# A hybrid decoder layer on one core: 24 transpositions of the identity ahead of the first rows

## The chip, the core and the metric

The kernel runs on one core of one Trainium2 chip. A core has five engines that run side by side, each through its own list of instructions, and wait for one another by semaphores: TensorE (PE) for matrix products and transpositions, its weight loads shown as PEld; VectorE (DVE) and ScalarE (ACT) for work on rows; GpSimd (POOL); and SyncE (SP), which here issues the transfers between DRAM and the on-chip memory SBUF. PE writes into PSUM, which has eight banks of 128 x 512 float32. The metric is the time of one execution on the device in microseconds (us).

## The reference

One decoder layer over 1024 positions of 1024 channels, with 16 learned "meta" rows put in front, all in float32:

```python
h = concat([meta, x])
hn = rms_norm(h, norm1_gain)
q, k, v, u = split(hn @ w_in)            # 512, 512, 512, 1024 columns
attn = diff_attention(q, k, v, ...)      # 4 heads, causal: softmax_1 - lam * softmax_2
conv = conformer_conv(u, ...)            # GLU, causal depthwise conv of 31 taps, LayerNorm, swish
h = h + concat([attn, conv]) @ w_out
a = relu(rms_norm(h, norm2_gain) @ w_up)
h = h + (a * a) @ w_down
return h[16:]
```

## The kernel before

Every matrix product is done on pairs: a float32 operand is split into a high part and a low part of the type that PE multiplies fast, and `three` (L317 to L321) issues high x high (L319), high x low (L320) and low x high (L321) into the same PSUM bank. The splitting takes ACT for the high part (L128 for activations, L138 for weights) and DVE for the low part (L129, L139).

At the start the rows come in as tiles: `mraw` with the 16 meta rows, and `xs` with eight tiles of 128 rows (L167, L215). `norm_tile` (L178) handles one: ACT squares the row and sums it (L182), POOL forms the reciprocal root (L124, L125), DVE scales the tile in place (L185), and PE transposes it in two halves of four 128 x 128 blocks each (L190, tile `xtr`, against the identity `ident`). Each half has a PSUM bank. The banks come from `trp`, a pool of two, but those of x tile 2 (`XPA`, L46) come from `pa`, the pool of six for products, tag `mm`. A bank is free again once ACT has copied its high part and DVE its low part (into `xm` for the meta rows, into `xT` for x). Meanwhile the weight rows `w_in` arrive in pieces `raw` of 128 x 512, with four buffers, and are split to `w`. The first products are `pu` (260 columns each: two x tiles and four meta columns), then `pq` for k, q and v, then the attention, the output projection and the feed-forward, whose second half (`py`, `px` with `pair`) fills the last third of the time.

`ident` is made by POOL at the very start (a memset and an affine_select in a helper, masks.py:197 and 199); all transpositions need it.

The order on each engine isn't that of the text. The kernel is recorded as it is written, and a scheduler then places the instructions on the engines by a model of their times (`schedule_with_timeline_sim=True`), within the limits that the pools' buffers and the data set. A new instruction can therefore move others, on any engine, anywhere behind it.

Of the kernel before, what the change touches and what calls it, by code (L numbers as in the profile page):

```python
# [9 lines left out]
F32 = mybir.dt.float32  # L10
# [6 lines left out]
P = 128  # L17
# [11 lines left out]
LATER = -200000  # L29
LOOK = 2  # L30
UQB = 2
FIN = 3
VPOS = (3,4)
APOSN = (3, 6)
# [25 lines left out]
def hybrid_layer_kernel(  # L60
# [18 lines left out]
    V, S, T, G = nc.vector, nc.scalar, nc.tensor, nc.gpsimd  # L79
# [9 lines left out]
    pa = ps_a.__enter__()  # L89
# [10 lines left out]
    def tr_bank(name):  # L100
# [7 lines left out]
    ident = cp.tile([P, P], F32, tag="ident", name="ident")  # L108
# [4 lines left out]
    G.memset(maskb, 0.0)  # L113
    G.affine_select(out=maskb, in_=maskb, compare_op=ALU.is_ge, fill=MASKED, base=0,
                    pattern=[[-1, P]], channel_multiplier=1)

    mhalf = cp.tile([P, 8], F32, tag="mhalf", name="mhalf")
    G.memset(mhalf, -0.5)
# [385 lines left out]
    def qstack(i, h, pool=None):  # L504
# [11 lines left out]
        for q in range(4):  # L516
            T.transpose(bank[:, q, :], qtf[:, q * P:(q + 1) * P], ident)
        uq = pool.tile([P, 4, P], F32R, tag=f"uq{h}", name=f"uq{h}") if pool else ap.tile([P, 4, P], F32R, tag="uq", name="uq", bufs=UQB)
        S.activation(uq, bank, AF.Copy)
# [231 lines left out]
    for n in range(-1, len(units) + BLAG):  # L751
# [20 lines left out]
        if n >= BLAG:  # L772
            i, h = units[n - BLAG]
            values(i, h, mixed.pop(0))
            if h == NH - 1:
                done.append((n + FIN, i, state["osb"], state["oss"]))
            if done and (n >= done[0][0] or n - BLAG == len(units) - 1):
# [457 lines left out]
```

## Time and profile before

| | us |
|---|---|
| three timed runs | 1132.49, 1133.85, 1135.59 |
| median | 1133.85 |
| the profiled execution | 1134.65 |
| its span, first to last instruction | 1132.5 |
| PE busy | 1098.7 (97%) |
| DVE busy | 814.8 (72%) |
| ACT busy | 618.5 (55%) |
| POOL busy | 142.3 (13%) |

All times below are counted from the first instruction of the profiled execution. PE's shares by stage tell where it waits; the waits themselves stand as "idle before, and what ended it" behind an instruction. An instruction's duration runs from its start to its end, and on PE, ACT and DVE the next one can start before that, so the distance of two starts is what a queue pays for one of them.

### The profile page before, as it was taken

Reading aid. Unit: us, or ns where it says so; the run is one execution under the profiler, and the core shown is the slowest. Engines: PE = TensorE matmul, PEld = TensorE weight load, DVE = VectorE, ACT = ScalarE, POOL = GpSimd, SP = SyncE. Lnnn points to the kernel's source line nnn. Section 1 sums busy time; section 2 is a strip of 40 time slices with the busy share of each in tenths; the row PEclk is TensorE's granted clock in tenths of the full one; section 3 lists DMA queues with packets and bytes.
Section 4 is the critical chain, followed back from the end, with each engine's and each line's share of the span. In section 5 each row is a group of like instructions: output and inputs, shape, how many; then the busy total and the mean of one; then the engine's idle time right before and its main releaser. Section 6 shows DMA issues by size and latency. Waiting matters only on the chain.

```text
span 1132.5 us, 15738 instructions
## 1 busy us (share of the span) xinstructions
PE 1098.7 (97%) x5696; PEld 925.3 (82%) x5696; DVE 814.8 (72%) x1354; ACT 618.5 (55%) x1379; POOL 142.3 (13%) x156
## 2 busy tenths in 40 slices
PE   6999999999999998997999999999999999999998
PEld 6999788877788877785888888878878888888887
DVE  7699899977888778689797878677657545356340
ACT  8521465447667676577767676676655333323320
POOL 3000564313001342250000000000000000000000
PEclk9999999999999999998999999999999999999999
DMA  7320011000222311384399996979399666465600
GB/s 269 118 76 1 1 38 38 29 10 19 75 71 97 131 66 57 110 271 140 130 330 322 311 339 238 331 252 328 148 340 384 245 256 219 190 229 201 220 38 37
DMA packets 87821, 189.92 MB, mean 168 GB/s; under 512 B 7472, under 2 KB 27184, under 8 KB 82112
## 3 DMA queue, kind: packets, MB, share of 16 engines
q1 hardware_dynamic: 87744, 188.92, 47.4%
q8 instruction: 44, 0.72, 0.3%
q14 instruction: 33, 0.27, 0.1%
HBM read 129.39 MB, written 59.51 MB: 167 GB/s over the span
## 4 chain that ended last, share of the span: by engine, by line
PE 81%; DVE 7%; DMA 5%; ACT 4%; issue 1%; POOL 1%; SPq 0%; POOLq 0%; DVEq 0%; ACTq 0%
PE px L321 7%; PE px L320 7%; PE px L319 7%; PE py L319 6%; PE py L320 6%; PE py L321 6%; PE pu L319 3%; PE pu L321 3%; PE pu L320 3%; PE pq L320 3%; PE pq L319 3%; PE pq L321 3%; PE ops L620 2%; PE pw L321 2%; PE pw L320 2%; PE pw L319 2%
## 5 line engine op out<-in xcount | busy, mean ns | idle before, releaser
L809 DVE TENSOR_TENSOR pair<-rv,pair 128x2048 fp32r<-128x2048 f32 x56 | 126.8, 2288 | 112.2 <-ACT pair L808 112.2
L808 ACT ACTIVATE pair<-rv 128x2048 fp32r<-128x2048 f32 x56 | 105.2, 1912 | 162.6 <-PE py L321 80.4
L319 PE MATMUL py<-pair 128*128 128x512 f32 x256 | 99.6, 389 | 0.0
L320 PE MATMUL py<-pair 128*128 128x512 f32 x256 | 99.6, 389 | 0.0
L321 PE MATMUL py<-pair 128*128 128x512 f32 x256 | 99.6, 389 | 0.0
L319 PE MATMUL px<-pair 128*128 128x512 f32 x192 | 74.8, 390 | 0.5 <-ACT pair L808 0.5
L320 PE MATMUL px<-pair 128*128 128x512 f32 x192 | 74.7, 389 | 0.0
L321 PE MATMUL px<-pair 128*128 128x512 f32 x192 | 73.8, 390 | 0.2 <-DVE pair L809 0.2
L320 PE MATMUL pu<-xT,w 128*128 128x260 f32 x256 | 72.1, 284 | 0.0
L319 PE MATMUL pu<-xT,w 128*128 128x260 f32 x256 | 71.4, 285 | 0.0
L321 PE MATMUL pu<-xT,w 128*128 128x260 f32 x256 | 71.4, 283 | 0.0
L894 ACT ACTIVATE wr<-wr,gains 128x256 f32<-128x256 f32 x128 | 54.8, 497 | 27.3 <-DMA wr<-in_w_up 26.7
L321 PEld LDWEIGHTS py<-pair 128*128 128x128 f32 x256 | 48.0, 188 | 10.1
L319 PEld LDWEIGHTS py<-pair 128*128 128x128 f32 x256 | 48.0, 188 | 10.0
L320 PEld LDWEIGHTS py<-pair 128*128 128x128 f32 x256 | 48.0, 188 | 9.9
L320 PE MATMUL px<-hnt,wp 128*128 128x512 f32 x128 | 51.1, 399 | 3.9 <-DVE hnt L809 3.9
L812 DVE TENSOR_TENSOR wdr<-wdr 128x1024 f32<-128x1024 f32 x32 | 39.1, 1221 | 20.4 <-DMA wdr<-in_w_down 20.2
L319 PE MATMUL px<-hnt,wp 128*128 128x512 f32 x128 | 50.7, 398 | 0.9 <-ACT sn L941 0.8
L321 PE MATMUL pq<-w,xT 128*128 128x512 f32 x128 | 50.9, 398 | 0.0
L319 PE MATMUL pq<-w,xT 128*128 128x512 f32 x128 | 50.9, 397 | 0.0
L320 PE MATMUL pq<-w,xT 128*128 128x512 f32 x128 | 50.8, 397 | 0.0
L321 PE MATMUL px<-hnt,wp 128*128 128x512 f32 x128 | 50.8, 397 | 0.0
(301 smaller groups left out, 3187.2 us busy)
## 6 DMA issues: line engine op xcount, KB each, us to landing
rv<-as SPq DMA_DIRECT2D x28, 1024.0 KB, 6.6
wr<-in_w_up SPq DMA_DIRECT2D x32, 512.0 KB, 5.0
as<-a SPq DMA_DIRECT2D x64, 256.0 KB, 4.9
wdr<-in_w_down SPq DMA_DIRECT2D x8, 2048.0 KB, 9.5
ws<-wdr SPq DMA_DIRECT2D x32, 512.0 KB, 4.4
rv<-ws SPq DMA_DIRECT2D x16, 1024.0 KB, 4.9
as<-as SPq DMA_DIRECT2D x48, 256.0 KB, 3.9
rv<-in_w_down SPq DMA_DIRECT2D x12, 1024.0 KB, 6.2
```

The source lines that it names most:

```text
L319: T.matmul(ps, st[0], mv[0], start=first, stop=False, skip_group_check=more)
L320: T.matmul(ps, st[0], mv[1], start=False, stop=False, skip_group_check=more)
L321: T.matmul(ps, st[1], mv[0], start=False, stop=last, skip_group_check=more)
L620: T.matmul(ops, u[:, 0, b, :], vb.rearrange("p a e -> p (a e)"), start=b == 0, stop=False)
L808: S.activation(hi, src, AF.Copy)
L809: (eng or V).tensor_tensor(out=lo, in0=src, in1=hi.bitcast(F32), op=ALU.subtract)
L812: eng.tensor_tensor(out=out, in0=a, in1=b, op=ALU.subtract)
L894: S.activation(r[:, k, :], r[:, k, :], AF.Copy, scale=gains[:, 1, 4 * j + k:4 * j + k + 1])
```

## The change

A constant `WAKE = 24` is added, and between the mask and `mhalf` in the setup a PSUM bank named `awake` is taken from `pa`, the pool of six. 24 transpositions of the identity by the identity, 128 x 128 in float32, are written into the four quarters of that bank in turn. Nothing reads it.

```diff
--- before.py
+++ after.py
@@ -29,6 +29,7 @@
 LATER = -200000
 LOOK = 2
 UQB = 2
+WAKE = 24
 FIN = 3
 VPOS = (3,4)
 APOSN = (3, 6)
@@ -113,6 +114,11 @@
     G.memset(maskb, 0.0)
     G.affine_select(out=maskb, in_=maskb, compare_op=ALU.is_ge, fill=MASKED, base=0,
                     pattern=[[-1, P]], channel_multiplier=1)
+
+
+    awake = pa.tile([P, 4, P], F32, tag="mm", name="awake")
+    for k in range(WAKE):
+        T.transpose(awake[:, k % 4, :], ident, ident)
 
     mhalf = cp.tile([P, 8], F32, tag="mhalf", name="mhalf")
     G.memset(mhalf, -0.5)
```

The changed file has these lines six further down (L190 of before is L196 of after). Names carry a buffer number that differs between the two builds; `xT_108` of before is `xT_133` of after, the pair of x tiles 0 and 1, and `w_186` is `w_211`, the first four weight pieces.

On PE the 24 stand at the head of the list, ahead of the meta rows' transpositions. The rows behind them are moved too. DVE before, from the scaling of x tile 0 to that of x tile 1 and three weight pieces:

```order
L185 TENSOR_SCALAR xs_102<-xs_102,rs 128x1024
L129 TENSOR_TENSOR xm<-xtr,xm 128x4x16 x2
L202 CAST xT_108<-xm 128x8x4
L202 CAST xT_109<-xm 128x8x4
L202 CAST xT_110<-xm 128x8x4
L202 CAST xT_111<-xm 128x8x4
L202 CAST xT_108<-xm 128x8x4
L202 CAST xT_109<-xm 128x8x4
L202 CAST xT_110<-xm 128x8x4
L202 CAST xT_111<-xm 128x8x4
L185 TENSOR_SCALAR xs_102<-xs_102,rs 128x1024
L139 SCALAR_TENSOR_TENSOR w_186<-raw,gains,w_186 128x512 x3
```

DVE after, the same part:

```order
L191 TENSOR_SCALAR xs_127<-xs_127,rs 128x1024
L145 SCALAR_TENSOR_TENSOR w_211<-raw,gains,w_211 128x512
L191 TENSOR_SCALAR xs_127<-xs_127,rs 128x1024
L145 SCALAR_TENSOR_TENSOR w_211<-raw,gains,w_211 128x512
L135 TENSOR_TENSOR xm<-xtr,xm 128x4x16
L145 SCALAR_TENSOR_TENSOR w_211<-raw,gains,w_211 128x512
L135 TENSOR_TENSOR xm<-xtr,xm 128x4x16
L208 CAST xT_133<-xm 128x8x4
L208 CAST xT_134<-xm 128x8x4
L208 CAST xT_135<-xm 128x8x4
L208 CAST xT_136<-xm 128x8x4
L145 SCALAR_TENSOR_TENSOR w_211<-raw,gains,w_211 128x512
```

The two copies of the meta rows' low parts (`xm`), which followed the scaling of x tile 0, now have one weight piece, x tile 1 and a second weight piece ahead of the first and a third piece ahead of the second; the eight casts come after, with the fourth piece among them. ACT is moved in the same way; before, from the Squares of the meta rows on:

```order
L182 ACTIVATE junk,ss<-mraw 16x1024
L182 ACTIVATE junk,ss<-xs_102 128x1024 x2
L128 ACTIVATE xm<-xtr 128x4x16 x2
L138 ACTIVATE w_186<-raw,gains 128x512 x3
L128 ACTIVATE xT_108<-xtr 128x4x128
L138 ACTIVATE w_186<-raw,gains 128x512
L128 ACTIVATE xT_108<-xtr 128x4x128
```

ACT after:

```order
L188 ACTIVATE junk,ss<-mraw 16x1024
L188 ACTIVATE junk,ss<-xs_127 128x1024 x2
L144 ACTIVATE w_211<-raw,gains 128x512 x2
L134 ACTIVATE xm<-xtr 128x4x16
L144 ACTIVATE w_211<-raw,gains 128x512
L134 ACTIVATE xm<-xtr 128x4x16
L144 ACTIVATE w_211<-raw,gains 128x512
L188 ACTIVATE junk,ss<-xs_127 128x1024
L134 ACTIVATE xT_133<-xtr 128x4x128 x2
```

The copies of `xm` stood behind the second x tile's Square; now two weight pieces stand ahead of the first and one between them, and the Square of x tile 2 is ahead of tile 0's copies. On SP the four pieces of the second half of these weights (L133), which followed all x tiles, now stand one by one between the x tiles 4 to 7.

Further on, up to the beginning of the feed-forward, rows are exchanged in many places on PE, DVE and ACT; in the last third the order is the same on all engines. One such place, in the attention, where the third block's result is transposed (`otr`, L640). PE before, with the last value products (`ops`) of a head ahead of it:

```order
L620 MATMUL ops<-vs_2913,u 128x256
L621 MATMUL ops<-vs_2913,u 128x128
L640 MATMUL otr<-ident,osb 128x128 x4
L517 MATMUL qtr<-ident,qt 128x128 x2
L607 MATMUL atr<-ident,pt 128x128
L517 MATMUL qtr<-ident,qt 128x128 x2
L620 MATMUL ops<-vm,u 128x256
L621 MATMUL ops<-vm,u 128x128
L620 MATMUL ops<-vs_2691,u 128x256
```

PE after, with the same `otr` in the eighth row:

```order
L523 MATMUL qtr<-ident,qt 128x128 x4
L544 MATMUL sps<-kst_1587,uq 128x264
L545 MATMUL sps<-kst_1587,uq 128x264
L544 MATMUL sps<-kst_1587,uq 128x264
L545 MATMUL sps<-kst_1587,uq 128x264
L547 LDWEIGHTS identb
L547 MATMUL sps<-maskb,identb 128x128
L646 MATMUL otr<-ident,osb 128x128 x4
L613 MATMUL atr<-ident,pt 128x128
L626 MATMUL ops<-vm,u 128x256
```

The output transposition now stands behind two groups of scores (`sps`); the query transpositions (`qtr`), which stood behind it on both sides of `atr`, have gone ahead.

## Rows read from the trace of the kernel before

**Rows 1.** The page: busy us, share of the span and instructions of each engine.

```profile
PE 1098.7 (97%) x5696; PEld 925.3 (82%) x5696; DVE 814.8 (72%) x1354; ACT 618.5 (55%) x1379; POOL 142.3 (13%) x156
```

**Rows 2.** Busy time by stage: stretch and length, engines, granted clock, DMA share, GB/s.

```profile
0.00:17.30 17.30, 8.06 (x38) 6.79 (x39) 11.35 (x33) 14.56 (x28) 7.72 (x23) 1.00 0.90 328
17.30:60.00 42.70, 42.70 (x361) 42.70 (x361) 32.35 (x71) 22.87 (x41) 2.92 (x6) 1.00 0.41 124
60.00:200.00 140.00, 140.00 (x851) 122.99 (x851) 132.46 (x238) 57.35 (x290) 49.41 (x28) 1.00 0.11 31
200.00:515.00 315.00, 301.51 (x1797) 253.41 (x1795) 252.44 (x568) 204.87 (x550) 82.27 (x99) 0.99 0.26 87
515.00:536.00 21.00, 15.26 (x54) 11.42 (x55) 19.92 (x28) 15.04 (x27) 0.00 (x0) 0.84 0.45 146
536.00:1132.50 596.50, 591.18 (x2603) 487.99 (x2602) 366.30 (x422) 303.84 (x446) 0.00 (x0) 1.00 0.67 242
```

**Rows 3.** Timeline of PE: start, length, line, tiles, count, idle before and releaser.

```profile
5.76 1.03 PE L190 MATMUL xtr<-ident,mraw 16*128 16x16 f32 x8 [5.76 <-DVE mraw L185]
8.01 1.97 PE L190 MATMUL xtr<-ident,xs 128*128 128x128 f32 x8 [1.22 <-DVE xm L129]
12.10 4.30 PE L190 MATMUL xtr<-ident,xs 128*128 128x128 f32 x16 [2.12 <-DVE xT L129]
16.05 1.22 PE L319 MATMUL pu<-xT,w 128*128 128x260 f32 x4
17.07 0.34 PE L320 MATMUL pu<-xT,w 128*128 128x260 f32 x1
```

**Rows 4.** Transpositions up to 20 us (min/median/max ns), and four later ones.

```profile
L190 PE MATMUL xtr<-ident,xs x32: 270/421/477, 8.0 to 19.9; 128*128 128x128 f32 x32
...
18.81 0.60 PE L190 MATMUL xtr<-ident,xs 128*128 128x128 f32 x4
```

**Rows 5.** Timeline of POOL, SP, ACT and DVE; the raw row is a DMA issue's landing.

```profile
1.17 0.29 POOL masks.py:199 TENSOR_SCALAR_AFFINE_SELECT ident<-ident 128x128 f32<-128x128 f32 x1
2.57 1.85 SPq L133 DMA_DIRECT2D raw<-in_w_in  x4
...
raw<-in_w_in SPq DMA_DIRECT2D x1, 256.0 KB, 5.0
...
7.36 0.32 ACT L128 ACTIVATE xm<-xtr 128x64 fp32r<-128x64 f32 x2
7.70 2.02 ACT L138 ACTIVATE w<-raw,gains 128x512 fp32r<-128x512 f32 x3
7.74 0.35 DVE L129 TENSOR_TENSOR xm<-xtr,xm 128x64 fp32r<-128x64 f32 x2
8.00 0.77 DVE L202 CAST xT<-xm 128x32 fp32r<-128x32 f32 x8
8.71 0.75 DVE L185 TENSOR_SCALAR xs<-xs,rs 128x1024 f32<-128x1024 f32 x1
9.38 2.07 DVE L139 SCALAR_TENSOR_TENSOR w<-raw,gains,w 128x512 fp32r<-128x512 f32 x3
11.36 0.68 DVE L129 TENSOR_TENSOR xT<-xtr,xT 128x512 fp32r<-128x512 f32 x1
14.29 0.22 DVE L269 TENSOR_TENSOR csum<-cw 128x60 f32<-128x60 f32 x1
```

**Rows 6.** Busy time in two pauses, columns as in rows 2.

```profile
399.00:403.00 4.00, 2.38 (x17) 1.76 (x17) 4.00 (x9) 2.65 (x6) 3.20 (x4) 0.99 0.24 90
403.00:406.40 3.40, 3.40 (x18) 3.29 (x18) 0.29 (x2) 3.15 (x12) 2.23 (x3) 0.52 0.00 0
526.80:530.80 4.00, 0.14 (x1) 0.00 (x0) 4.00 (x7) 1.93 (x4) 0.00 (x0) 0.80 0.72 232
530.80:536.00 5.20, 5.14 (x12) 4.12 (x13) 4.12 (x7) 2.34 (x6) 0.00 (x0) 0.50 0.49 159
```

**Rows 7.** PE's waits from 200 to 515, the longest single one: total, times, longest.

```profile
PE qtr L517 <- DVE msb L563: 1.7, 1, 1.7
```

## The prediction

> **What bounds the kernel now.** I read the page's busy shares first, then the busy time by stage, and then the first 20 us and two pauses instruction by instruction. TensorE (PE) is busy for 1098.7 of 1132.5 us [rows 1], so a change can give back at most the 33.8 us in which PE stands. The stages say where these lie: 17.30 - 8.06 = 9.24 us before 17.3 us, none from there to 200 us, 315.00 - 301.51 = 13.49 us in the attention (200 to 515), 21.00 - 15.26 = 5.74 us where the feed-forward begins (515 to 536), 596.50 - 591.18 = 5.32 us in all the rest [rows 2].
>
> The added work lies in the first of these stages, so what ends the waits there counts. PE waits for its first tile to be scaled until 5.76, for the first PSUM bank of the transpositions to be emptied by VectorE (DVE) until 8.01 and again until 12.10; its first product is issued at 16.05, and the first one that needs a low part (L320) at 17.07 [rows 3]. PE also runs at half pace there: eight transpositions take 1.97 us at 8.01, of which the last is 0.42 long, so (1.97 - 0.42) / 7, some 0.215 us apart; at 18.81 four take 0.60 us, so (0.60 - 0.27) / 3 = 0.11 us apart [rows 3, 4]. [...]
>
> **The change, part by part.** *The 24 transpositions.* They need the identity alone, which POOL has finished at 1.17 + 0.29 = 1.46 [rows 5]. At half pace they end at 1.5 + 24 x 0.215 = 6.7, at full pace at 1.5 + 24 x 0.11 = 4.1. The eight transpositions of the meta rows, which began at 5.76, so begin between 5.76 and 6.7, up to 0.9 us late. ScalarE (ACT) did not read them before the end of its second Square, near 7.4, and DVE not before 7.74 [rows 5], so by itself this costs nothing. The bank comes from the pool of six for products; its only writer is PE, which is long past it when the bank comes round: nothing, and at worst one wait for PE itself, which is in order anyway.
>
> *What they would give, if nothing else moved.* Between 12.10 and 17.2 PE ran 16 transpositions and 4 products at half pace, that is 16 x (0.215 - 0.11) = 1.65 us, and about half of the 1.02 us from 16.05 to 17.07, more than at full pace [rows 3, 4]. Together that is the end on the good side: -2.2 us.
>
> *The order.* The build's scheduler has placed everything anew, taking the meta rows to be late. On ACT two pieces of weights now go ahead of the first copy xm, and a third ahead of the second; on DVE likewise, with a scaling of xs in between. I walk this with the old durations. The first piece lands at 2.57 + 5.0 = 7.57 and ACT takes 2.02 / 3 = 0.67 us for each. DVE: weights 8.3 to 9.0, xs 9.0 to 9.7 (0.67 apart), weights 9.7 to 10.4, xm to 10.6 [rows 5]. Only then is the meta bank free, so x tile 0 is transposed from 10.6 (first half) and, one weight piece later, 11.4 (second half), where it was 8.01. Eight small casts (0.77) and the fourth piece (0.67) then hold DVE until 12.85, three tiny ones until about 13.1 (csum, one of that kind, takes 0.22 and they overlap), and the low part of tile 0's first half (0.68) ends at 13.75: tile 1 begins at 13.8, where it was 12.10. Then xs is scaled by 14.65, tile 2 is transposed from 14.7 (its bank is of the product pool), the second half of tile 0 is split until 15.3, and tile 1's second half follows tile 2. At full pace PE is through with these and with the four L319 at 16.5, at half pace at 18.2. The low part of tile 1's first half comes after csum, a weight piece and an xs (15.3 + 0.15 + 0.67 + 0.67, and 0.68 for itself) and ends at 17.45. So the first L320, which stood at 17.07 with the same work behind it, now stands at 17.5 with a full clock (+0.4) and at 18.2 with half a clock.
>
> *Which clock.* Between about 7.7 and 13.8 PE now has only eight transpositions, some 0.9 us of work. In the attention the clock fell while PE was busy for 2.38 of 4 us, and stood at 0.52 in the next 3.4 us; in the other pause it fell after PE had stood since 526.8, and read 0.50 from 530.8 to 536 [rows 6]. So whatever the 24 transpositions bring is probably given back before 13.8. Then PE works without a pause from 14.7. In the kernel before the pace doubled 17.2 - 16.05 = 1.15 us after the first product [rows 3]; at half pace the first product now stands at 17.2, so the same gives 18.4. That is half pace up to the first L320 at 18.2 and 0.2 us beyond, where before it was 0.1: 18.2 - 17.07 + (0.2 - 0.1) / 2, or +1.2 us.
>
> [...]
>
> For the start I take +0.8, between +0.4 and +1.2, with ends at -2.2 and, if the pace doubles some 1.5 us later still, +2.0. That no new wait follows rests on the cover after 17.3: PE was busy for all of 42.70 us, DVE for 32.35 and ACT for 22.87 [rows 2], so both have 10 us to spare. If a split of 0.68 us comes too late there, it costs that once or twice, at most 1.4 us.
>
> *SyncE's queue.* The second half's weight pieces now stand between the x tiles 4 to 7, one each, and each waits for its buffer, so a tile behind it is issued later. These tiles are used after 17.3, under the same cover: nothing, at most the 1.4 us already counted.
>
> *The attention and beyond.* There all queues have the same instructions in another order, transpositions and splits standing some rows earlier or later; from the feed-forward on the orders differ by single instructions, and the last third is the same. The 13.49 us of waits there are many short ones, the longest 1.7 us; the pause at 527, 4.00 - 0.14 us, lies behind it [rows 2, 6, 7]. I can derive no sign: 0, with one wait of 1.7 us either way as its usual size.
>
> The sum: the profiled execution took 1134.65 us, 2.15 more than its span, and lies 0.8 above the median of 1133.85. 1134.65 + 0.8 + 0 = 1135.45 on its scale, so 1133.85 + 0.8 = 1134.7 for the median. A difference of 0.3%, 3.4 us, is about what a measurement of this kernel can tell from none.
>
> **Rivals.** *The attention gets a pause more (slower).* The place is that of the kind at 399, where the output transpositions wait for DVE: 4.00 - 2.38 = 1.62 us standing and then 3.4 us at half clock, a loss of 1.7 [rows 6]. One more such place is +3.3, with the start's +0.8 and one wait of 1.7 it is 1133.85 + 5.8 = 1139.6; alone 1138.0. It decides once a wait is long or dense enough that the clock falls, since that doubles its price. For it: the new order puts these output transpositions right behind the scores, with no value products ahead of them. Against it: as many products are left to put elsewhere.
>
> *The attention loses that pause (faster).* In the same place the new order lets the value products of the earlier head go before. If the pause and the clock's fall go, and the longest wait of 1.7 too [rows 7]: 1133.85 + 0.8 - 3.3 - 1.7 = 1129.7. For it speaks only that the place is rearranged.
>
> *The clock rises early and stays (does what it says).* Then the start is worth between -2.2 and +0.4: 1131.7 to 1134.3, say 1133.0. Against it speak the six nearly idle microseconds.
>
> *The clock never notices the transpositions.* Then the first pieces run at half pace as walked above: 1133.85 + 1.2 = 1135.1. For it: PE was at half pace through all the transpositions from 5.76 on [rows 3]; against it: they had pauses of 1.22 and 2.12 us between them.
>
> **How the numbers follow.** The forecast, a start at +0.8 and an attention within 1.7 us, 0.45; clock early 0.08; clock unmoved 0.10; a pause more 0.22; a pause less 0.15. The first three lie within 0.3%, so 0.63 for no change, 0.15 for faster (below 1130.45) and 0.22 for slower (above 1137.25). The forecast's own range is 1131 to 1137 (the start's ends and one wait). The range of 8 in 10 reaches into the two others, to their nearer prices: 1130.0 to 1139.0.
>
> **What would show it.** Right: 24 transpositions from about 1.5 us, 0.21 us apart at first; the first x tile transposed near 10.6; the first L320 between 17.4 and 18.3; PE then without a wait up to 200 us. A fall in the pace between 8 and 14 us, or a granted clock of 0.5 there, would show that the warmth is given back; if the transpositions at 14.7 stand 0.11 us apart, it was not. The standing time from 200 to 515 against 13.49 us decides between the first two rivals. I am wrong if the first L320 stands before 16.5 or after 19, or if that standing time moves by more than 3 us.

## The result: 0.6% slower

| | before | after |
|---|---|---|
| median of 14 runs each, us | 1134.22 | 1141.74 |
| lowest to highest, us | 1132.49 to 1141.79 | 1138.68 to 1143.8 |
| ratio, 95% interval | | 1.0056, 1.0044 to 1.0067 |
| the profiled execution, us | 1134.65 | 1140.35 |
| its span, us | 1132.5 | 1138.6 |

The forecast was 1134.7 us, no change. A second series of the changed kernel gave 1142.96 us and a ratio of 1.0066 (1.0047 to 1.0085). All lines of the text stand 6 further down: L319, L320, L321 are L325, L326, L327 now, L808 is L814.

The page of the changed kernel answers to [rows 1]. Below the busy row stands the row of DMA queue q8, of the kind "instruction" (the other queue of that kind, q14, has 33 packets before and after): queue, packets, MB, share.

```profile
PE 1103.6 (97%) x5720; PEld 929.4 (82%) x5720; DVE 813.5 (71%) x1354; ACT 616.2 (54%) x1379; POOL 143.4 (13%) x156
...
q8 instruction: 45, 0.74, 0.3%
```

PE has 24 matmuls more. In the kernel before the same row of q8 read as follows:

```profile
q8 instruction: 44, 0.72, 0.3%
```

One packet more, each 16 KB: in the kernel before that is a packet for every 5696 / 44, some 129 matmuls. That its packets go with PE's list is what the runs below show: with nothing added but 24 small matmuls on PE, the packet that came between 838 and 842 us came between 831 and 834. That row turns out to be the most telling one of the page.

Busy time by stage, columns as in [rows 2]; the last stage is 6 us longer than before.

```profile
0.00:17.30 17.30, 11.06 (x57) 10.17 (x57) 10.62 (x31) 13.72 (x26) 6.13 (x23) 0.78 0.86 307
17.30:60.00 42.70, 42.70 (x351) 42.70 (x350) 31.08 (x68) 23.52 (x43) 2.95 (x7) 0.97 0.42 133
60.00:200.00 140.00, 140.00 (x859) 123.52 (x858) 132.47 (x236) 56.98 (x290) 49.91 (x27) 1.00 0.11 31
200.00:515.00 315.00, 300.19 (x1793) 251.39 (x1793) 249.74 (x569) 200.58 (x543) 84.36 (x101) 1.00 0.26 86
515.00:536.00 21.00, 14.18 (x61) 10.49 (x60) 21.00 (x32) 16.44 (x31) 0.00 (x0) 0.98 0.44 144
536.00:1138.60 602.60, 595.43 (x2609) 491.15 (x2608) 368.58 (x425) 304.93 (x450) 0.00 (x0) 0.99 0.67 240
```

PE stands for 14.81 us in the attention, 1.32 more than in [rows 2], and for 7.17 us after 536, where it was 5.32. Both differences are small beside 6 us, and stages cut at fixed times hide what moves across their borders. A better measure is the start of one and the same PE instruction in the two traces. The changed kernel is late by 1.94 us at the end of the first projections (113 us in before), by 2.55 at 423, by 2.62 at 574, by 3.27 at 822 and by 6.07 at 867 and from there to the end. So nearly half of it, 2.80 us, is lost where the feed-forward changes over from the up to the down products, a stretch in which all engines have the instructions of before in the order of before.

PE's first 20 us, answering to [rows 3]:

```profile
1.52 5.12 PE L121 MATMUL awake<-ident 128*128 128x128 f32 x24 [1.52 <-POOL ident masks.py:199]
6.57 0.66 PE L196 MATMUL xtr<-ident,mraw 16*128 16x16 f32 x8
10.96 1.97 PE L196 MATMUL xtr<-ident,xs 128*128 128x128 f32 x8 [3.73 <-DVE xm L135]
13.92 3.69 PE L196 MATMUL xtr<-ident,xs 128*128 128x128 f32 x16 [0.99 <-DVE xT L135]
17.26 1.22 PE L325 MATMUL pu<-xT,w 128*128 128x260 f32 x4
18.28 1.05 PE L196 MATMUL xtr<-ident,xs 128*128 128x128 f32 x4
18.98 0.57 PE L326 MATMUL pu<-xT,w 128*128 128x260 f32 x1
```

The first L326 stands at 18.98, where L320 stood at 17.07 [rows 3]: +1.91. The eight meta transpositions take 0.66 us instead of 1.03, 0.06 apart and not 0.11, so the pace had doubled by then; the next eight take 1.97 again, 0.21 apart. The clock, in four pieces of this stage, columns as in [rows 2]:

```profile
0.00:6.00 6.00, 4.48 (x21) 4.48 (x22) 1.27 (x3) 3.78 (x6) 2.28 (x13) 1.00 0.65 212
6.00:9.40 3.40, 1.24 (x13) 0.97 (x11) 1.46 (x3) 2.61 (x6) 1.74 (x4) 1.00 1.02 373
9.40:17.00 7.60, 5.04 (x23) 4.42 (x24) 7.60 (x27) 7.03 (x15) 1.89 (x5) 0.52 0.94 347
17.00:19.90 2.90, 2.90 (x15) 2.90 (x14) 2.90 (x5) 2.81 (x6) 0.81 (x3) 0.50 1.04 419
```

The first 1.00 can't be taken as it stands: up to 6.05 us the added transpositions start 0.21 us apart, like the eight from 10.96 on, over which the column reads 0.50. The second goes with the pace of the meta rows, and from 9.4, or a little later, to 19.9 the column reads half (0.52 and 0.50). The clock was raised and given back while PE stood until 10.96, and came for good 2.7 us later than in before, where the pace doubled at 17.2 (its products start 0.22 us apart up to 17.07 and 0.12 from 17.25 on, while the column reads 1.00 all along [rows 2]).

At the change-over, PE's longest wait from 545 to 870 us in the changed kernel, then in the kernel before (total, times, longest):

```profile
PE px L325 <- ACT pair L814: 2.2, 1, 2.2
```

```profile
PE px L319 <- ACT pair L808: 0.5, 1, 0.5
```

and the clock behind that wait in the changed kernel:

```profile
835.00:838.00 3.00, 1.91 (x9) 1.25 (x7) 2.29 (x1) 1.50 (x2) 0.00 (x0) 1.00 1.03 350
838.00:845.00 7.00, 5.88 (x19) 4.78 (x20) 2.74 (x2) 2.98 (x2) 0.00 (x0) 0.76 1.03 394
```

The wait is 1.7 us longer, and the clock then falls to half (0.50 from 839.2 to 842.4) for (1.00 - 0.76) x 7 / 0.5 = 3.4 us, in which the other 1.1 of the 2.80 us are lost. The longest wait of [rows 7], in the attention, is what it was:

```profile
PE qtr L523 <- DVE msb L569: 1.7, 1, 1.7
```

### The profile page after: what moved, and what is told of

Read it like the earlier page. It is cut to its first block, busy times and chain, and to the rows that moved or that the text cites. A ratio compares the mean times of both kernels' runs of the same rounds, so it can differ in the third digit from the quotient of the medians.

```text
span 1138.6 us, 15781 instructions
## 1 busy us (share of the span) xinstructions
PE 1103.6 (97%) x5720; PEld 929.4 (82%) x5720; DVE 813.5 (71%) x1354; ACT 616.2 (54%) x1379; POOL 143.4 (13%) x156
## 4 chain that ended last, share of the span: by engine, by line
PE 75%; DMA 8%; DVE 8%; ACT 6%; issue 2%; POOL 1%; SPq 0%; POOLq 0%; DVEq 0%; ACTq 0%
PE px L325 6%; PE px L326 6%; PE px L327 6%; PE py L325 6%; PE py L326 6%; PE py L327 6%; DMA wr<-in_w_up 4%; PE pu L325 3%; PE pu L327 3%; PE pu L326 3%; PE pq L325 3%; PE pq L326 3%; PE pq L327 3%; PE pw L326 2%; PE pw L325 2%
## 5 line engine op out<-in xcount | busy, mean ns | idle before, releaser
L815 DVE TENSOR_TENSOR pair<-rv,pair 128x2048 fp32r<-128x2048 f32 x56 | 126.7, 2288 | 112.6 <-ACT pair L814 112.6
L814 ACT ACTIVATE pair<-rv 128x2048 fp32r<-128x2048 f32 x56 | 105.1, 1911 | 165.6 <-PE py L327 80.8
L325 PE MATMUL py<-pair 128*128 128x512 f32 x256 | 99.6, 389 | 0.0
L326 PE MATMUL py<-pair 128*128 128x512 f32 x256 | 99.6, 389 | 0.0
L327 PE MATMUL py<-pair 128*128 128x512 f32 x256 | 99.6, 389 | 0.0
L325 PE MATMUL px<-pair 128*128 128x512 f32 x192 | 75.8, 395 | 2.2 <-ACT pair L814 2.2
L326 PE MATMUL px<-pair 128*128 128x512 f32 x192 | 75.5, 393 | 0.0
L327 PE MATMUL px<-pair 128*128 128x512 f32 x192 | 73.7, 389 | 0.0
L326 PE MATMUL pu<-xT,w 128*128 128x260 f32 x256 | 72.6, 286 | 0.0
L327 PE MATMUL pu<-xT,w 128*128 128x260 f32 x256 | 72.0, 283 | 0.0
L325 PE MATMUL pu<-xT,w 128*128 128x260 f32 x256 | 71.8, 285 | 0.0
L325 PEld LDWEIGHTS py<-pair 128*128 128x128 f32 x256 | 48.0, 188 | 10.1
L327 PEld LDWEIGHTS py<-pair 128*128 128x128 f32 x256 | 48.0, 188 | 10.0
L326 PEld LDWEIGHTS py<-pair 128*128 128x128 f32 x256 | 48.0, 188 | 9.9
L818 DVE TENSOR_TENSOR wdr<-wdr 128x1024 f32<-128x1024 f32 x32 | 39.1, 1222 | 22.0 <-DMA wdr<-in_w_down 21.8
L326 PE MATMUL px<-hnt,wp 128*128 128x512 f32 x128 | 50.7, 396 | 3.9 <-DVE hnt L815 3.9
L325 PE MATMUL px<-hnt,wp 128*128 128x512 f32 x128 | 50.5, 395 | 1.2 <-ACT sn L947 1.0
L326 PE MATMUL pq<-w,xT 128*128 128x512 f32 x128 | 50.9, 398 | 0.0
L325 PE MATMUL pq<-w,xT 128*128 128x512 f32 x128 | 50.7, 396 | 0.0
L327 PE MATMUL px<-hnt,wp 128*128 128x512 f32 x128 | 50.6, 395 | 0.0
L327 PE MATMUL pq<-w,xT 128*128 128x512 f32 x128 | 50.5, 395 | 0.0
```

Of the source, the lines that this page charges most:

```text
L325: T.matmul(ps, st[0], mv[0], start=first, stop=False, skip_group_check=more)
L326: T.matmul(ps, st[0], mv[1], start=False, stop=False, skip_group_check=more)
L327: T.matmul(ps, st[1], mv[0], start=False, stop=last, skip_group_check=more)
L814: S.activation(hi, src, AF.Copy)
L815: (eng or V).tensor_tensor(out=lo, in0=src, in1=hi.bitcast(F32), op=ALU.subtract)
L818: eng.tensor_tensor(out=out, in0=a, in1=b, op=ALU.subtract)
```

## The experiments

The change has three parts that can be told apart: the order the scheduler makes of it, 5 us of PE work near whose end, at about 6 us, the pace doubles, and 24 more instructions in PE's list. With 16 transpositions or 15 the scheduler kept the order of before, as the traces of those runs show on every engine. So each part can be had alone: the built program keeps its order, and a few lines behind the build take transpositions out of PE's list or put copies in. `MORE = {n: (a, b)}` stands for a full transpositions (128x128) and b small ones (of a 16x16 corner of the identity, some 0.03 us each: 24 of them take 0.80) ahead of the n-th of PE's own instructions, and a plain number for full ones alone: 0 is the first meta transposition, 8, 16 and 24 those of x tiles 0, 1 and 2. The diffs are cut to the lines that set a run apart; what reads `MORE` is left out. Where two kernels share a diff, each one's other values stand behind the #. Each ratio is to the kernel before as timed beside that run, with the 95% interval. The lines of the text stand 7 to 11 further down in these kernels (L808 is L815, L818 or L819).

**The order alone.**

```diff
+KEEP = 1
+    blk = next(b for b in nc.m.functions[0].blocks if len(b.instructions) > 1000)
+    aw = [i.name for i in blk.instructions if "out=[dt.float32@awake" in str(i)]
+    blk.instructions = [i for i in blk.instructions if i.name not in aw[KEEP:]]
```

> The changed program with 23 of its 24 transpositions taken out again after the scheduler had laid it out: the changed order on every engine, no work added on PE. Theory A (the order alone costs the time): 1.0045 to 1.0065 of the kernel before, the first L326 near 18 us or a little later at the half clock, PE 2 to 3 us late by the end of the projections and 5 to 7 us late at the end. Theory B (the transpositions cost it, by the clock that rises early and falls again): within 0.2% of before, PE less than 1 us late from 60 us on.

Measured: 1137.28 us, ratio 1.0012 (0.9999 to 1.0025). Neither theory holds whole: the time is as theory B has it, and the interval allows that the order alone costs nothing; but the trace is late where theory B has it on time. It has the later start (x tile 0 at 11.72, the first product at 18.00 where it was 16.05) and is 2.31 us late at the end of the projections.

**The transpositions alone, in the order of before.**

```diff
+WAKE = 16
+MORE = {0: 8}
```

> 24 transpositions of the identity ahead of the meta rows, but every engine in the order of the kernel before. Theory A (the order): 0.998 to 1.001 of before; the first pu product at 16.5 to 17.2 us. Theory B (the transpositions and the clock): 1.003 to 1.006, with the later half-clock stretches of the changed kernel (near 839 us) in place.

Measured: 1140.15 us, 1.0039 (1.0023 to 1.0055). The theory that the order explains everything fell here. The start is 0.72 us shorter than in before; in the trace 3.72 us are lost between 423 and 822, where single traces scatter (table below), and 2.51 at the change-over. There PE waits longer, though without the half-clock stretch that theory B expected near 839 (the clock is 1.00 from 822 to 870):

```profile
PE px L326 <- ACT pair L815: 3.0, 1, 3.0
```

**The clock kept up.**

```diff
+WAKE = 16
+MORE = {0: 8, 8: 6, 16: 28, 24: 26}
```

> The order of the kernel before with 24 transpositions ahead of the meta rows and 6, 28 and 26 more in the three waits behind them, so that PE does not stand between 1.5 and 17 us. If the clock that rose at 6.0 us in the changed kernel fell at 9.4 only because PE stood, it stays full here, tile 1 and 2 are transposed in 0.9 us each instead of 1.8, and the first pu product starts at 15.5 to 17.1 us: 0.5 to 2 us faster than before (0.998 to 0.9995). Rival: the projections wait for the split rows and weights all the same and nothing comes out (0.9995 to 1.0005), or the fillers hold up the real transpositions (1.001 to 1.003).

Measured: 1137.31 us, 1.0013 (0.9997 to 1.003). No gain: the projections end 0.78 us later than in before. Yet this kernel, with 84 transpositions, lost only 0.57 us at the change-over, where 24 lost 2.5. More of the same costs less, so it isn't the work that costs.

**The changed kernel once more.** No edit.

> The changed kernel once more, for a second trace. If the 2.8 us that it loses near 838 us come from its order, PE waits again for pair at L814 by about 2 us and the clock falls to half there; if that was a matter of one execution, the wait is near 0.5 us as before and PE is only about 3 us late at the end of the trace, while the timed ratio stays at 1.004 to 1.007.

Measured: 1142.96 us, 1.0066 (1.0047 to 1.0085). The second trace has the same wait, 3.0 us, and the same fall of the clock behind it, so the loss at the change-over is no matter of one execution.

**24 instructions without the work.** Set against PE's own progress, the kernels with 24 transpositions have a packet of q8 near 832 us, among the first weight loads of the down products, where those with none or one have it at 840 and the one with 84 at 850. Hence theory F.

```diff
+WAKE = 0
+TINY = 24
+    for k in range(TINY):
+        T.transpose(awake[:16, 3, :16], ident[:16, :16], ident[:16, :16])
```

> The order of the kernel before with 24 transpositions of a 16x16 corner of the identity ahead of the meta rows: as many PE instructions as in the changed kernel, hardly any PE work, all of it in a wait. Theory F (place of PE's instruction loads: the 16 KB packets of DMA queue q8 come every 128 or so matmuls, and 24 more matmuls move one of them from 840 us to about 832, among the first weight loads of the down products): the clock is as in before, PE waits 2 to 3 us for pair near 835 us instead of 0.5, and the time is 1.002 to 1.005 of before. Theory C (the clock that rises early and falls again, with what follows from it): 0.9990 to 1.0010, the wait at 0.5 to 1 us.

Measured: 1138.30 us, 1.0029 (1.0015 to 1.0044), as theory F has it. In its trace PE is 0.25 us late at 822 and 2.68 late from 867 on, and the clock is full from 16 us on (1.00 from 822 to 845, where the changed kernel has its fall) but for the pause at 531 to 535, which before has too. The wait at the change-over, and the packet in a window of 3 us (DMA queues, columns as above):

```profile
PE px L329 <- ACT pair L818: 2.9, 1, 2.9
```

```profile
q8 instruction: 1, 0.02, 2.0%
```

The window is 831 to 834 us. In the kernel before, the packet comes from 838 to 842 us. ACT's first splits of the down products, in the kernel before and then in this one (start, length, what ended the idle time):

```profile
829.61 1.92 ACT L808 ACTIVATE pair<-rv 128x2048 fp32r<-128x2048 f32 x1 [4.79 <-DMA rv<-in_w_down]
832.12 1.92 ACT L808 ACTIVATE pair<-rv 128x2048 fp32r<-128x2048 f32 x1 [0.60 <-DMA rv<-as]
```

```profile
830.47 1.92 ACT L818 ACTIVATE pair<-rv 128x2048 fp32r<-128x2048 f32 x1 [5.41 <-DMA rv<-in_w_down]
834.79 1.91 ACT L818 ACTIVATE pair<-rv 128x2048 fp32r<-128x2048 f32 x1 [2.40 <-DVE pair L819]
```

The split of the weights is 0.86 us late and that of the activations 2.67, of which 0.25 are the trace's lateness at 822. The splits wait for their 1 MB loads, and PE waits for the splits. The load that is late is the second one, of `as`; in the kernel before and in this one (KB, us from issue to landing):

```profile
rv<-as SPq DMA_DIRECT2D x1, 1024.0 KB, 8.0
```

```profile
rv<-as SPq DMA_DIRECT2D x1, 1024.0 KB, 10.4
```

It is issued at 824.33 and lands at 834.7, just ahead of the split. The row names DVE, whose own split ended at 834.7 too; but in the kernel before ACT began its second split at 832.12, while DVE's first ran to 833.85, so it is the load that ACT waits for.

**48 instead of 24.**

```diff
+WAKE = 0
+TINY = 12
+MORE = {8: (0, 36)}
```

> As the last, with 48 small transpositions, 12 ahead of the meta rows and 36 behind them, where PE waits. Theory F: the load that was moved to 832 us comes some 5 us earlier still, at 825 to 828, before the first of the weight loads; the wait for pair near 835 us is 0.5 to 1.5 us and the time 0.9990 to 1.0025 of before. Theory C: 0.9990 to 1.0010.

Measured: 1135.30 us, 1.0001 (0.9982 to 1.002). Twice the instructions, and the loss is gone. The packet now comes at 824.2, before the load of `as` is issued (826.2):

```profile
PE px L329 <- ACT pair L818: 0.9, 1, 0.9
```

**The full transpositions with the packet moved on,** in the order of before and in the changed one.

```diff
+MORE = {0: (9, 0), 8: (0, 4), 16: (0, 34)}   # WAKE = 15, TINY = 2
+MORE = {8: (0, 39)}                          # WAKE = 24, TINY = 1
```

> The order of before with the 24 full transpositions (1.0039 of before when alone) and 40 of a 16x16 corner behind them, 6 near the meta rows and 34 behind x tile 0, where PE waits. The clock rises early as with the 24 alone. Theory F: the instruction load is moved out of the first weight loads (to 820 to 826 us), the wait for pair goes back to 0.5 to 1.5 us: 0.9985 to 1.0020. Theory C: the early clock is still there, 1.003 to 1.006.

> The changed kernel (1.0056 to 1.0066 of before) with 40 transpositions of a 16x16 corner more, 1 ahead of the meta rows and 39 behind them, where PE waits until 10.9 us. Theory F: what is left is the order's cost at the start, 1.000 to 1.003. Theory C: 1.0045 to 1.007.

Measured: 1.0018 (1.0005 to 1.0032) and 1.0039 (1.0023 to 1.0055). The wait for pair goes from 3.0 to 1.4 us and from 2.2 or 3.0 to 1.2, with the packet at 821.1 and 822.7, and by the point values both kernels are some 0.2% faster for 40 instructions more, though the intervals overlap with those without the 40. The second lies above what F alone expected, and under what C did.

**128, one whole spacing of the packets.**

```diff
+MORE = {0: (0, 48), 8: (0, 20), 16: (0, 30), 24: (0, 18)}          # WAKE = 0, TINY = 12
+MORE = {0: (9, 0), 8: (4, 10), 16: (24, 20), 24: (22, 22)}         # WAKE = 15, TINY = 2
```

> The order of before with 128 transpositions of a 16x16 corner, spread over the four waits of PE before 16 us. The packets of DMA queue q8 come once in some 128 matmuls, so each stands where the one after it stood in before. Theory F: the instruction load near the change-over is back at about 840 us, the wait for pair is 0.4 to 1 us and the time 0.9985 to 1.0012 of before. A theory by which every matmul that is added at the start costs something: 1.004 or more, since there are five times as many as in the kernel with 24 small ones (1.0029).

> The order of before, 74 full and 54 small transpositions, 128 in all: 24 full ones ahead of the meta rows, the others in the three waits behind them, so that the clock that rises at 6 us has no reason to fall, with the instruction loads where they are in before. If both causes are understood, the start is 0.5 to 1.5 us shorter than in before, the change-over as in before, and the time 0.9980 to 1.0003. Rival: the fillers hold up the real transpositions, 1.0005 to 1.003.

Measured: 1.0019 (1.0006 to 1.0031) and 1.0014 (0.9998 to 1.003). At the change-over they lose 0.67 and 0.77 us, with waits of 1.1 and 1.2 and the packet at 843.0 and 840.5, about as expected, though both times come out 0.1% above theory F's ends. The second holds the clock from 4 us on, as its timeline shows by the pace (9 transpositions of 128x128 in 1.20 us, x tile 0 in 1.09 instead of 1.97):

```profile
1.52 3.21 PE L123 MATMUL awake<-ident 128*128 128x128 f32 x15 [1.52 <-POOL ident masks.py:199]
4.66 0.20 PE L125 MATMUL awake<-ident 16*16 16x16 f32 x2
4.80 1.20 PE L123 MATMUL awake<-ident 128*128 128x128 f32 x9
5.93 0.66 PE L200 MATMUL xtr<-ident,mraw 16*128 16x16 f32 x8
6.52 0.66 PE L123 MATMUL awake<-ident 128*128 128x128 f32 x4
7.11 0.41 PE L125 MATMUL awake<-ident 16*16 16x16 f32 x10
7.90 1.09 PE L200 MATMUL xtr<-ident,xs 128*128 128x128 f32 x8 [0.39 <-DVE xm L139]
```

and still its projections end 1.17 us later than in before, since the second half of tile 1 waits for its bank and the fillers behind it run late. The warm clock, the aim of such transpositions, has bought nothing in any of these kernels.

**The changed order with small ones.** These have the 24 or 48 instructions and the order, without the 5 us of work.

```diff
+MORE = {0: (0, 22)}             # WAKE = 24, TINY = 1, KEEP = 1 full one
+MORE = {0: (0, 10), 8: (0, 36)} # the same
```

> The changed order on all engines with 1 full and 23 small transpositions: as many PE instructions as in the changed kernel, without the 5 us of PE work that raise the clock. If order and instruction place add up (1.0012 and 1.0029 each alone), 1.003 to 1.005, with a wait of 2 to 3 us for pair; what is missing to the changed kernel's 1.0056 to 1.0066 is then the early clock's. If the early clock costs nothing, 1.0055 to 1.0065; if the place of the instruction loads costs nothing on this order, 1.000 to 1.0025.

> The changed order with 1 full and 47 small transpositions, 12 of the 48 ahead of the meta rows and 36 behind them: the place of the instruction loads of the old order with 48 small ones (1.0001 of before), 5 us earlier than in the changed kernel. Theory F with a share of the order's own: the wait for pair is 0.9 to 1.6 us, the time 1.001 to 1.004, clearly under the 1.0069 of the same order with 24. If the order's loss grows with every matmul that is added at the start, or 24 on this order cost what they cost for another reason than the load's place: 1.006 or more.

Measured: 1.0069 (1.0057 to 1.0081) and 1.0051 (1.0034 to 1.0068). The first is as slow as the changed kernel although the clock rises at no time before 17.8 (the meta rows take 1.03 us as in before, the next eight transpositions 1.97), so the early clock is not the cause. It also lies above all that I had expected of it: 1.0012 and 1.0029 don't add up to 1.0069. The second is less slow by 0.18%, with overlapping intervals, and lies between theory F's 1.004 and its rival's 1.006. The waits, first of these two and then of the other:

```profile
PE px L330 <- ACT pair L819: 2.8, 1, 2.8
```

```profile
PE px L330 <- ACT pair L819: 1.7, 1, 1.7
```

**All together.** Shift of PE's instructions against the trace of before, in us: at the end of the projections (113 us), and gained or lost from 113 to 423, 423 to 822 and 822 to 867 us of before. N is the number of transpositions added.

| order | N | ratio | to 113 | 113-423 | 423-822 | 822-867 |
|---|---|---|---|---|---|---|
| before | 24 small | 1.0029 | -0.49 | +0.53 | +0.21 | **+2.43** |
| before | 24 full | 1.0039 | -0.72 | +0.49 | +3.72 | **+2.51** |
| before | 48 small | 1.0001 | -0.74 | -0.95 | +3.55 | +0.47 |
| before | 24 full, 40 small | 1.0018 | +0.82 | -1.68 | +2.77 | +0.93 |
| before | 84 full | 1.0013 | +0.78 | -1.47 | -2.24 | +0.57 |
| before | 128 small | 1.0019 | +0.73 | -1.99 | +3.21 | +0.67 |
| before | 74 full, 54 small | 1.0014 | +1.17 | -1.90 | +0.53 | +0.77 |
| changed | 1 full | 1.0012 | +2.31 | +0.51 | +1.62 | +0.92 |
| changed | 24, 23 of them small | 1.0069 | +0.74 | +0.48 | +5.07 | **+3.45** |
| changed | 24 full (the change) | 1.0056 | +1.94 | +0.61 | +0.72 | **+2.80** |
| changed | the same again | 1.0066 | +1.33 | +2.07 | +1.63 | **+3.70** |
| changed | 48, 47 of them small | 1.0051 | +0.35 | +1.14 | +3.09 | +1.30 |
| changed | 24 full, 40 small | 1.0039 | +0.67 | +2.93 | -0.33 | +0.78 |

The clearest column is the last. It goes by N: 2.4 to 3.7 us at 24, 0.5 to 1.3 at any other number, whatever the order, the size of the transpositions and the clock at the start. Within the 24, the order of before loses 2.43 and 2.51, about what the wait for pair grew by (2.4 and 2.5), and its clock stays full there (1.00 from 822 to 870 in both). In all three traces of the changed order the clock falls to half behind the wait (0.51 from 843.8 to 847.3 in the one with 23 small ones), and they lose some 1.1 to 1.2 us more than their wait grew by.

The load of `as` goes with it. It takes 8.0 to 8.9 us in the nine traces with another number (before included) and 9.7 to 10.6 in the five with 24, the only ones in which a packet of q8 starts while that load is under way. A packet in a later load of 1 MB did not show like this: in the kernel before one comes at 840.1, within a load that took 12.4 us (828.46 to 840.84), the shortest of its kind in the 14 traces (12.4 to 13.4).

The other columns show less. All are shifts against one trace of the kernel before, and the two traces of the changed kernel already differ by 0.6, 1.5 and 0.9 us in them. The means of the first two are 1.2 and 1.3 us in the changed order, 0.2 and -1.0 in that of before, but the groups overlap. In the first, the same small or full 24 are 1.2 to 2.7 us later in the changed order, while with 40 more there is no difference. In the second, the orders differ by 2.1 and 4.6 us with 48 and 64 transpositions, and by nothing at 24 but for the changed kernel's second trace. The third depends on neither; single traces differ there by up to 7 us.

The times, averaged: with the order of before 1.0013 where N isn't 24 and 1.0034 where it is; with the changed one 1.0034 and 1.0064. By these means the order and the number 24 are worth 0.2 to 0.3% each. The means hide that the changed order alone took 1.0012 and with 48 took 1.0051 (1.0034 to 1.0068), though it lost only 1.30 us at the change-over; what made that difference is open. Whether the 24 are full or small, that is whether the clock rises early, makes no difference that these times can tell.

No kernel tried is faster than the one before; the nearest is the one with 48 small ones, at 1.0001.

## Why the prediction was wrong

*The step that failed* is that the 24 transpositions cost nothing by themselves ("so by itself this costs nothing"). I priced them as work, in a wait, behind the cover of ACT and DVE, and as work they do cost nothing. They also lengthen PE's list, and the packets of q8 come at other places of the work behind them: the one at 840.1 us in the kernel before comes at 835.0 in the changed one, though that one is 3.27 us late at 822. At that number of instructions, whatever their size, the change-over takes longer: +2.80 us of the 6.07 in the trace and about 0.25% of the time. I had written of the last third that it "is the same", and taken 0 for it. The order was the same; the place of the packets wasn't. No rival had it, and the time lies above both prices of the slower one, 1138.0 and 1139.6. The row of q8 was on the page, and I hadn't read it. My signs of being wrong did not fire either: the first L326 stands at 18.98, under 19, and the standing time of the attention moved by 1.32, under 3. Both look at what lies ahead of 515 us.

Three slips in the working changed nothing. (1.97 - 0.42) / 7 is 0.22 and not 0.215; 16 x (0.215 - 0.11) is 1.68 and not 1.65; and the start's ends with one wait give 1130.0 to 1137.6 and not 1131 to 1137.

*The first 20 us.* The walk along ACT and DVE held: tile 0 at 10.96 (10.6 forecast), the warmth given back between 7.7 and 13.8 (the clock read 0.52 from 9.4 on), the half-pace branch. Its size was too small: +1.91 at the first L326 and +1.94 at 113 us against +0.8, just inside the end of +2.0. The clock doubled at 19.9 and not at 18.4: I had taken the time from the first product to the rise from one trace, 1.15 us, where the changed kernel showed 2.6. In the second trace all of this stands some 0.6 us earlier (tile 0 at 10.39, the rise near 19.3, again 2.6 behind the first product), which gave +1.33: the start varies from one execution to the next.

*The attention.* "I can derive no sign", 0 within 1.7. The changed kernel lost 0.61 us from 113 to 423 in one trace and 2.07 in the other, the order of before with the same 24 lost 0.49. Some 0.35 of it arise by 281 in every trace of the changed order and in none of the other; for the rest the traces show no cost of the order that stands clear of their scatter. The two rivals about the pause at 399 both failed in an instructive way. Here are the stretches before and behind the clock's fall in the kernel before, then the same instructions' in the changed one:

```profile
280.80:402.80 122.00, 118.31 (x780) 102.84 (x779) 101.72 (x228) 83.17 (x201) 22.55 (x22) 1.00 0.28 94
402.80:423.20 20.40, 20.04 (x133) 17.67 (x133) 14.82 (x43) 15.57 (x49) 6.25 (x10) 0.92 0.15 52
```

```profile
283.10:405.40 122.30, 117.76 (x776) 102.12 (x774) 99.57 (x227) 81.00 (x198) 19.91 (x20) 1.00 0.28 91
405.40:425.75 20.35, 19.25 (x135) 16.73 (x135) 15.96 (x43) 15.46 (x49) 9.77 (x14) 1.00 0.20 66
```

The fall of the clock in [rows 6] is gone, 1.00 for 0.92, as the rival that was faster wanted, and the stretch is no shorter: PE stands for 1.10 us there instead of 0.36. So at half pace PE had been busy, it seems, in a time in which it would else have waited. Nor is this the order's doing: of the 14 traces only that of the kernel before has the fall near 403, and the seven others in its order have none. In the kernel with 24 small ones, the same two stretches of [rows 6] read:

```profile
399.00:403.00 4.00, 3.07 (x24) 2.41 (x22) 3.96 (x7) 2.54 (x6) 4.00 (x5) 1.00 0.55 168
403.00:406.40 3.40, 2.71 (x23) 2.67 (x24) 1.78 (x6) 3.00 (x8) 1.63 (x2) 1.00 0.00 0
```

So a price taken from one pause of one trace was no price of the order. A pause more came too, but near 838, where I had not looked.

*The rival that the clock never notices the transpositions* is contradicted: PE had done nothing but transpositions when the pace doubled, near 6 us in the changed kernel (the meta rows in 0.66 us and not 1.03) and near 4.5 in the kernel with 128 (15 transpositions of 128x128 in 3.21 us, the 9 from 4.80 on in 1.20).

*Still open.* That the loss at the change-over goes by N is shown, and that with N = 24, alone among the numbers tried, a packet of q8 comes within the load of `as`, which then takes some 1.8 us longer on the mean. That the packet holds up the load is argued from this; how one packet, some 1 us of one DMA engine's time (2.0% of 16 engines in 3 us), would do so is not shown. In the kernel with 24 small ones the first split is already 0.6 us late before the packet comes, but that is no matter of N: the first load takes 5.9 us in the one trace of before and 6.0 to 7.0 in all 13 others. No run has 24 transpositions spread over the waits, or 48 in one place, so their number was not told apart from their place among the first instructions. Where the changed order costs what it costs, beyond the start, was not tried.

## What to carry to other kernels

Where instructions are added on an engine, look at the loads too: here 24 small ones on PE brought a packet of q8 from 838-842 us to 831-834, into a load of 1 MB that took 10.4 us and not 8.0. When a change that adds idle work costs time far from its place, look where the instruction queue's packets fall among the loads that PE waits for, and try another number of instructions before looking for another cause. Where a scheduler places the work, undo the order and the work separately, in the built program, since each can cost as much as the other. Take a second trace of the kernel before, too: here all shifts hang on one, and its fall of the clock at 403 stood in no other. And read one instruction's start in both traces, stage by stage, before explaining anything: busy time by stage showed 1 to 2 us where 3 were lost.

## What the runs showed of the hardware

- 24 transpositions of a 16x16 corner against 48 (12 in the same place, 36 in the next wait), all else alike: 2.43 and 0.47 us lost 820 us later, ratios 1.0029 and 1.0001.
- One and the same load of 1 MB took 9.7 to 10.6 us in the five traces in which a 16 KB packet of the instruction queue q8 came while it was under way, and 8.0 to 8.9 in the nine others.
- TensorE's pace doubled with nothing but transpositions ahead of it: 24 in 5.12 us, 0.21 apart at first and 0.11 at the end, and behind them the eight of the meta rows in 0.66 us against 1.03. Where PE then stood from 7.2 to 10.96 us the clock read 0.50 when PE went on: the next eight took 1.97 us against 1.09 in the kernel that kept PE going.
- The column of the granted clock read 1.00 over the first 6 us of the changed kernel and the first 17.3 us of the one before, though those of 128x128 started 0.21 us apart there, as from 10.96 on in the changed kernel, where it read 0.50; where the column read 1.00 later, at 18.81 in the kernel before, they started 0.11 apart. The distance of two equal instructions told the pace in these traces where the column did not.
